# One over rms by token taken from its row through memory, and a reordering around a last projection, in a decoder layer on one core

## The chip, the core and the metric

The kernel runs on one core of one Trainium2 chip. The time is device microseconds of one execution; for before it is the median of three runs. TensorE (PE) multiplies, with its weight loads (PEld) beside it; VectorE (DVE), ScalarE (ACT) and GpSimd (POOL) work elementwise; SyncE (SP) issues most transfers, POOL and ScalarE some. Each engine runs its own queue of instructions in order and waits for others through semaphores.

## The reference

One decoder layer in float32: 512 tokens, width 1024, 256 memory tokens, FFN hidden width 2816.

```python
def rms_norm(x, g):
    var = jnp.mean(x * x, axis=-1, keepdims=True)
    return x * lax.rsqrt(var + EPS) * g

h = rms_norm(x, norm_mix)
q_a, k_a, v_a, u_b, gate_b, gate_c, g_a, g_b = split(h @ w_in)
# A: strictly causal stick-breaking attention, 8 heads of 64
# B: gate_b * causal_depthwise_conv3(gate_c * u_b)
merged = sigmoid(g_a) * (o_a @ w_branch_a) + sigmoid(g_b) * (y_b @ w_branch_b)
x = x + merged @ w_mix_out
# softmax attention over memory, 4 heads of 256
x = x + memory_cross_attention(rms_norm(x, norm_mem_q), rms_norm(mem, norm_mem_kv), ...)
gate, up = split(rms_norm(x, norm_ffn) @ w_ffn_in)
x = x + (silu(gate) * up) @ w_ffn_out
return rms_norm(x, norm_final)
```

There are five norms: first (mixer), memory, second (queries to the memory), third (FFN) and final. In the kernel 1/rms is not multiplied into the activations. It stays out of the matmuls and is applied to their results.

## The kernel before, in words

Activations lie turned, channels on partitions and tokens along the free dimension: 8 tiles of 128x512. To keep float32 accuracy every operand of a matmul is split into a high part in fp32r (made by a cast on ScalarE, or on VectorE at attention's weights) and the low rest (a subtraction on VectorE), and a product is three matmuls: high·high, high·low, low·high. The names end in `h` and `l`: `wh`, `wl` for weights from a raw tile `wr` (`load_w`), `xgh`, `xgl` for activations times the norm's gain. A weight tile passes through SyncE's load, ScalarE's cast and VectorE's subtraction; the pools have four buffers of each, so the next cast waits until TensorE has left an older tile.

**Norms.** Squares are added up per channel tile on VectorE into `acc` (`acc0`, `accm` for the memory). `squares_mean` splits `acc` into `acch` and `accl` and gives two ways to the mean over the channels, both by a matmul with the matrix `mean_r`: `along` yields the mean of every token along a row, the same on all partitions (`varb`, two matmuls of 128x512, or 128x256 for the memory), and `by_token` yields one column per 128 tokens, tokens on partitions (`var`, two matmuls of 128x2 per 128 tokens: eight, or four for the memory). `rstd_of` makes 1/rms of it by Ln and Exp on ScalarE and one Newton step on VectorE. The first norm uses both: the row `r0b` scales projections that lie turned, the column `r0` scales v, whose tokens lie on partitions. The memory norm uses both (`rm`, `rmb`), the second only a column `r1`, the third a row, that `turn_r2` also turns into a column `rt` for the final stage: POOL stores the row to DRAM and loads it back as four columns.

**Order of the work.** v of all tokens (L260), `stacked` splits v; then stick-breaking attention in steps, with projections, convolution, gates, memory norm (at step MEAN_AT) and memory projections as filling; per step `scores` makes z, `weights` the exponent `a` and its split `ah`, `al` (L385, L386), `values` multiplies by v. POOL masks `e` and `a` (L329). Then the branch projections `br` and the mixed output (`residual`, tiles `r`), which also makes x1's activations, their squares and `mean1`. While `residual` and what follows run, POOL adds four parts of FFN output weights (`pre`, L467, `weight_sums`); its first loads wait for a copy of x1's first activation. Then per memory head: `mem_q` (two query tiles `mq` of 24 matmuls each), scores `sc`, softmax with `r1s`, `om`; `residual` again; then the FFN.

The FFN's up and gate products are done by a scheme of seven products per hidden tile pair (banks z, v, y; weights `wf`), and so is the output projection (tiles `p`, weights `w01`, `w23`, `w46` and `wq`, forms `f01`, `fh`, `f26`, `f45` of the hidden activations). `second` makes `sb` from y and frees y's bank; `evict` multiplies by the row of the third norm (part 0), applies Silu (1), multiplies gate and up (2). `out_cast` loads and casts a weight, `rest_of` makes its low part, `out_pair` does both. In the last loop of the projection each iteration has six or more products per pair (`run`), the next weights, and one of eight output tiles from `groups`: its residual is turned by TensorE (`turned`), and one iteration later `settle` adds it on VectorE; for the tiles (0,0) and (1,0), `l`, ScalarE squares them right then.

In the FFN's stages the order on TensorE, ScalarE and VectorE is the order in the code. Before them a scheduler orders each engine's queue, from the code's order and the dependences.

Of the kernel before, what the change touches and what calls it, by code (L numbers as in the profile page):

```python
# [13 lines left out]
P = 128  # L14
# [29 lines left out]
def hybrid_layer(ctx: ExitStack, tc: tile.TileContext, xT_d, memT_d, cols_d, wv_d, win_d,  # L44
# [28 lines left out]
    def f(ap):  # L73
        return ap.bitcast(F32)
# [7 lines left out]
    def otile(s):  # L82
        return mmtile(s, po, "o")
# [92 lines left out]
    def squares_mean(acc, n):  # L176

        parts = unit("acch", n * P), unit("accl", n * P)
        nc.vector.tensor_copy(parts[0], acc)
        nc.vector.tensor_tensor(out=parts[1], in0=acc, in1=f(parts[0]), op=ALU.subtract)  # L180

        def by_token(s, tables=()):

            vp = otile("var")
            for t in range(n):
                for i in range(2):
                    nc.tensor.matmul(vp[:, 2 * t:2 * t + 2], parts[i][:, t * P:(t + 1) * P],
                                     mean_r[:, 0:2], start=i == 0, stop=i == 1)
            return rstd_of(vp[:, 0:2 * n].rearrange("p (t two) -> p t two", two=2)[:, :, 0], n, s,
                           tables)  # L190

        def along(s, tables=(), bank=otile):

            vp = bank("varb")[:, :n * P]
            for i in range(2):
                nc.tensor.matmul(vp, mean_r, parts[i], start=i == 0, stop=i == 1)
            return rstd_of(vp, n * P, s, tables)

        return by_token, along


    xg, wv = [], []
    acc0 = tmp("acc")
# [33 lines left out]
        lead.append(square)  # L237
    mean0 = squares_mean(acc0, TT)

    def stacked(src, scale, odd):  # L240
# [5 lines left out]
        nc.scalar.activation(hi, src, AF.Copy, scale=scale)  # L246
        nc.vector.scalar_tensor_tensor(out=lo, in0=src, scalar=scale, in1=f(hi), op0=ALU.mult,
                                       op1=ALU.subtract)
        return u


# [1 line left out]
    for k in range(KD):  # L253

        terms = ((0, 0), (0, 1), (1, 0))
        for some in ((term,) for term in terms) if k == 0 else (terms,):
            for t in range(TT):
                sl = slice(t * P, (t + 1) * P)
                for a, b in some:
                    nc.tensor.matmul(vps[t], xg[k][a][:, sl], wv[k][b],  # L260
                                     start=k == 0 and (a, b) == (0, 0),
                                     stop=k == KD - 1 and a == 1)
    r0b, r0 = mean0[1]("r0b"), mean0[0]("r0")
    v = [[stacked(vps[t], r0[:, t:t + 1], h) for h in range(2)] for t in range(TT)]


    def project(col):
# [101 lines left out]
    def weights(p, kt):  # L369
        c0, n, d = span(kt)  # L370
        av[p, kt] = []
        for h in range(2):
            z = zs[p, kt][h][:, :n]
            if kt < TT - 1:
                off = span(kt + 1)[0] - c0
                for part in rest[p, kt, h]:
                    nc.tensor.matmul(z[:, off:], neg1, part, start=False, stop=False,
                                     skip_group_check=True)
            for part in sp[p, kt, h]:
                nc.tensor.matmul(z, negtri, part, start=False, stop=True, skip_group_check=True)  # L380
# [4 lines left out]
            nc.vector.tensor_copy(ah, a)  # L385
            nc.vector.tensor_tensor(out=al, in0=a, in1=f(ah), op=ALU.subtract)  # L386
            av[p, kt].append((ah, al))

    def values(p, kt):
# [48 lines left out]
    for i in range(len(steps) + 1):  # L438
        if i in MEM_AT:
            mem_square(MEM_AT.index(i))  # L440
        if i == MEAN_AT - 4:
            mean = squares_mean(accm, MT)
        if i == MEAN_AT:
            rm, rmb = mean[0]("rm"), mean[1]("rmb")
        while fill and n_fill - len(fill) < (i + 1) * n_fill / len(steps):
            g, *args = fill.pop(0)
            g(*args)
        if i + 1 < len(steps):
            scores(*steps[i + 1])
        if i < len(steps):  # L450
            weights(*steps[i])
        if i > 0:
            values(*steps[i - 1])
# [148 lines left out]
    def mem_q(h):  # L602
        got = []
        for j in range(2):
            w = load_w(wmq_d[2 * h + j])
            ps = mmtile("mq")
            gemm(ps, w, x1g)
            got.append(split(ps, "mq"))
        return got

    q_next = mem_q(0)
    r1 = mean1[0]("r1", log_exp_tables(sigmoid))
    r1s = cpool.tile([P, TT], F32, tag="r1s", name="r1s")
    nc.vector.tensor_scalar(out=r1s, in0=r1, scalar1=(D // MH) ** -0.5, scalar2=None, op0=ALU.mult)
    for h in range(MH):
# [173 lines left out]
    rt = cpool.tile([P, TT], F32, tag="rt", name="rt")  # L789
    nrt = cpool.tile([P, TT], F32, tag="nrt", name="nrt")  # L790

    def turn_r2():

        row = dpool.tile([1, S], F32, tag="row", name="row")
        nc.gpsimd.dma_start(row, r2b[0][0:1, :])
        nc.gpsimd.dma_start(rt, row.rearrange("o (t p) -> p (o t)", p=P))
        nc.gpsimd.tensor_scalar(out=nrt, in0=rt, scalar1=-1.0, scalar2=None, op0=ALU.mult)

    forms, ows = {}, {}

# [98 lines left out]
    def w01(j):  # L899
        return j, wq(j), 0, 1  # L900
# [20 lines left out]
    with tc.manual_schedule(engines={mybir.EngineType.PE, mybir.EngineType.Activation,  # L921
# [6 lines left out]
        for n, (m, i) in enumerate(uses):  # L928
            if (m, i) == (1, 0):
                product(banks[m]["z"], m, i, range(KP - 1, KP))  # L930
            elif n > 2:
                product(bank_of(m, i), m, i)
            if i == 4:
                reads(m, i)
            else:
                if i == 1 and m > 0:
                    second(m - 1)
                reads(m, i)
            if n + AHEAD < len(uses):
                ffn_form(*uses[n + AHEAD])  # L940
            if n + AHEAD + SUM_AHEAD < len(uses):
                ffn_raw(*uses[n + AHEAD + SUM_AHEAD])
            if (m, i) == (0, 6):
                r2b[0] = mean2[1]("r0b", bank=mmtile)
                turn_r2()

            if i == 0 and m > 1:
                evict(m - 2, 0)
            elif i == 4 and 0 < m < NF - 1:
                evict(m - 1, 1)  # L950
            elif i == 1 and m > 1:
                evict(m - 2, 2)
            if (m, i) == (NF - 2, 6):
                evict(m, 0)
                evict(m, 1)
                x3 = half_form(3, 0, 0)
# [97 lines left out]

        def onto(out_, p, t, old, sign=1):
            nc.vector.scalar_tensor_tensor(out=out_, in0=p,
                                           scalar=(rt if sign > 0 else nrt)[:, t:t + 1], in1=old,
                                           op0=ALU.mult, op1=ALU.add)

        ys = {}  # L1060
# [39 lines left out]
        for j in range(NJ - 2):  # L1100
            run(4, j)
            if j == 0:
                uv = [plus("uv", res[2][s2], u[s2]) for s2 in range(2)]
                res[5] = [ztile("p5") for _ in range(2)]
            settle()
            act_third(j + 2)
            run(6, j)
            out_pair(*w46(j + 2))
            if 0 < j < BEHIND + 1:
                run(5, j - 1)  # L1110
            out_one(j + 1)
            if j < len(groups):
                pending.append((*groups[j], turned(*groups[j])))
# [137 lines left out]
```

## Time and profile before

| | |
|---|---|
| median of three runs | 862.02 us (861.31 to 862.38) |
| profiled execution | 862.09 us, of which 860.4 us span |
| granted TensorE clock | 0.998 |
| TensorE busy | 846.9 us, 98% |
| VectorE busy | 656.9 us, 76% |
| ScalarE busy | 460.2 us, 53% |
| POOL busy | 152.2 us, 18% |
| moved by DMA | 139.54 MB, mean 162 GB/s |

A row of the profile names the engine, the line of the kernel, the operation, and the tiles that it writes and reads (`out<-in`). In a view in time the first number is the start in us and the second the length; brackets at the end give how long the engine had stood idle before the instruction, and what ended that. Matmuls overlap: a 128x512 one is listed with 0.39 us, yet the next starts 0.227 us later, so a gap is read from starts. "Chain" is the chain of work that ended last, followed back from the end through whatever released each step.

### The profile page before, as it was taken

What the parts mean: (1) busy time and instruction counts of PE and PEld (TensorE: products, weight loads), DVE (VectorE), ACT (ScalarE), POOL (GpSimd) and SP (SyncE); (2) the same over time, 40 slices, a digit from 0 to 9 for tenths busy, and PEclk for the clock granted to TensorE, in tenths of its full rate; (3) what the DMA queues carried; (4) which work ended last, traced back from release to release, by engine and by line L of the source; (5) the groups of instructions that cost most, each with busy time, mean ns of one, the idle gap of its engine ahead of it and who ended that gap; (6) DMA issues with size and microseconds to landing.
All of it is one profiled execution on the core that took longest, in us unless ns stands there. A gap on an engine that the chain in (4) does not pass through costs nothing.

```text
span 860.4 us, 12842 instructions
## 1 busy us (share of the span) xinstructions
PE 846.9 (98%) x4840; PEld 737.6 (86%) x4840; DVE 656.9 (76%) x1082; ACT 460.2 (53%) x846; POOL 152.2 (18%) x183
## 2 busy tenths in 40 slices
PE   9999999999999999999999999999999999999995
PEld 7878888887888889888888789999999999888884
DVE  7768898986665766577555689888887888899877
ACT  7566676666332354533344566654455555576644
POOL 0021221111556540064000011111111110000001
PEclk9999999999999999999999999999999999999999
DMA  8332212225588766566441435767777773366542
GB/s 294 122 111 86 86 62 74 74 75 171 202 297 304 283 231 197 172 237 238 135 111 50 103 74 140 186 173 183 184 181 189 189 178 97 127 227 204 171 167 98
DMA packets 48574, 139.54 MB, mean 162 GB/s; under 512 B 4608, under 2 KB 6656, under 8 KB 45696
## 3 DMA queue, kind: packets, MB, share of 16 engines
q1 hardware_dynamic: 39008, 103.82, 36.6%
q0 software_dynamic: 9216, 34.61, 15.4%
q8 instruction: 38, 0.62, 0.3%
q10 hardware_dynamic: 288, 0.28, 0.1%
q14 instruction: 24, 0.20, 0.1%
HBM read 125.07 MB, written 13.63 MB: 161 GB/s over the span
## 4 chain that ended last, share of the span: by engine, by line
PE 95%; DVE 3%; ACT 1%; issue 1%; POOL 0%; ACTq 0%; DVEq 0%; POOLq 0%
PE z L727 15%; PE p L992 9%; PE pr L155 8%; PE pr L154 8%; PE pr L156 8%; PE y L727 7%; PE v L727 4%; PE r L155 3%; PE r L156 3%; PE r L154 3%; PE v L260 3%; PE br L154 2%; PE mq L156 2%; PE br L155 2%; PE mq L155 2%; PE mq L154 2%
## 5 line engine op out<-in xcount | busy, mean ns | idle before, releaser
L149 ACT CAST wh<-wr 128x1024 fp32r<-128x1024 f32 x84 | 88.0, 1052 | 165.4 <-issue 73.0
L150 DVE TENSOR_TENSOR wl<-wr,wh 128x1024 fp32r<-128x1024 f32 x84 | 110.4, 1316 | 36.7 <-ACT wh L149 36.6
L155 PE MATMUL pr<-xgl,wh 128*128 128x512 f32 x288 | 112.4, 390 | 0.0
L154 PE MATMUL pr<-xgh,wh 128*128 128x512 f32 x288 | 112.3, 390 | 0.0
L156 PE MATMUL pr<-xgh,wl 128*128 128x512 f32 x288 | 112.2, 390 | 0.0
L467 POOL TENSOR_TENSOR pre<-pre 128x512 f32<-128x512 f32 x44 | 71.8, 1636 | 33.7 <-DMA pre<-in_w_ffn_out_dram 31.4
L696 POOL DMA_DIRECT2D ws<-in_w_ffn_in_dram x22 | 26.5, 1206 | 256.1 <-DVE wf L717 122.9
L727 PE MATMUL z<-xdh,wf 128*128 128x256 f32 x352 | 70.5, 283 | 0.2 <-ACT sb L748 0.2
L156 PEld LDWEIGHTS pr<-xgh,wl 128*128 128x128 f32 x288 | 54.1, 188 | 11.2
L154 PEld LDWEIGHTS pr<-xgh,wh 128*128 128x128 f32 x288 | 54.1, 188 | 11.0
L155 PEld LDWEIGHTS pr<-xgl,wh 128*128 128x128 f32 x288 | 54.1, 188 | 11.0
L748 ACT COPY sa<-z 128x256 f32<-128x256 f32 x44 | 16.4, 372 | 79.3 <-PE z L727 78.4
L727 PEld LDWEIGHTS z<-xdh,wf 128*128 128x128 f32 x352 | 58.0, 192 | 0.5 <-ACT sb L748 0.4
L717 DVE TENSOR_TENSOR wf<-s,wf 128x512 fp32r<-128x512 f32 x44 | 30.3, 691 | 25.7 <-ACT wf L716 25.6
L727 PE MATMUL z<-xdl,wf 128*128 128x256 f32 x176 | 49.8, 283 | 0.0
L810 DVE TENSOR_TENSOR wl<-wr,wh 128x1024 fp32r<-128x1024 f32 x33 | 40.3, 1223 | 4.7 <-ACT wh L877 4.7
L877 ACT CAST wh<-wr 128x1024 fp32r<-128x1024 f32 x33 | 34.5, 1049 | 6.4 <-DMA wr<-sums 4.3
L727 PE MATMUL y<-xoh,wf 128*128 128x256 f32 x176 | 35.4, 284 | 0.7 <-DVE sb L758 0.7
L727 PE MATMUL z<-xch,wf 128*128 128x256 f32 x176 | 35.4, 284 | 0.1
L727 PE MATMUL y<-xch,wf 128*128 128x256 f32 x176 | 35.4, 283 | 0.0
L727 PE MATMUL v<-xoh,wf 128*128 128x256 f32 x176 | 35.4, 283 | 0.0
L727 PE MATMUL z<-xf,wf 128*128 128x256 f32 x264 | 35.4, 283 | 0.0
(333 smaller groups left out, 2422.3 us busy)
## 6 DMA issues: line engine op xcount, KB each, us to landing
wr<-in_w_in_dram SPq DMA_DIRECT2D x36, 512.0 KB, 3.5
pre<-in_w_ffn_out_dram POOLq DMA_DIRECT2D x11, 1024.0 KB, 8.5
sums<-pre POOLq DMA_DIRECT2D x11, 1024.0 KB, 4.9
ws<-in_w_ffn_in_dram SPq DMA_DIRECT2D x22, 512.0 KB, 3.7
wg<-in_w_ffn_in_dram SPq DMA_DIRECT2D x22, 512.0 KB, 4.3
ws<-in_w_ffn_in_dram POOLq DMA_DIRECT2D x22, 512.0 KB, 6.3
wr<-sums SPq DMA_DIRECT2D x22, 512.0 KB, 4.5
wr<-in_w_ffn_out_dram SPq DMA_DIRECT2D x16, 512.0 KB, 4.0
```

Of the source, the lines that this page charges most:

```text
L149: after(nc.scalar.copy(h2, raw), lead[-1:])
L150: lows.append(nc.vector.tensor_tensor(out=l2, in0=raw, in1=f(h2), op=ALU.subtract))
L154: nc.tensor.matmul(ps, a[0], b[0], start=start, stop=False, **kw)
L155: nc.tensor.matmul(ps, a[0], b[1], start=False, stop=False, **kw)
L156: nc.tensor.matmul(ps, a[1], b[0], start=False, stop=stop, **kw)
L467: nc.gpsimd.tensor_tensor(out=t[:, a, :], in0=t[:, a, :], in1=t[:, b, :], op=ALU.add)
L696: nc.gpsimd.dma_start(s13, a[:, 0:4:3, :], accum_op=ALU.add)
L717: nc.vector.tensor_tensor(out=w[:, 1, :], in0=raw, in1=f(w[:, 0, :]), op=ALU.subtract)
L727: nc.tensor.matmul(ps[:, :HS], a, b, start=i < 3 and k == 0 and j == 0, stop=k == KP - 1 and j == 2, skip_group_check=True)
L810: nc.vector.tensor_tensor(out=lo, in0=src, in1=f(hi), op=ALU.subtract)
L877: nc.scalar.copy(hi, raw)
L992: nc.tensor.matmul(res[i][s2], a[:, ts], b, start=j == 0 and n == 0, stop=j == NJ - 1 and n == 2)
```

## The change

1. `by_token` goes. `squares_mean` now gives `along` and a new `turned`, which copies the row of means with ScalarE, stores it to DRAM and loads it back as columns (both on SyncE), and makes 1/rms of the columns. The common part is `turned_row`.
2. First norm: only the row is made, and `r0` is read from `r0b` by POOL's two transfers. v is split without it; `r0` is multiplied into attention's weights, where `ah` becomes a TENSOR_SCALAR and `al` a SCALAR_TENSOR_TENSOR.
3. Memory norm: the same, `rm` from `rmb` by two transfers of POOL.
4. Second norm: `turned`, and it is called ahead of `mem_q(0)`, where the column was made behind it.
5. End of the gate and up products: `second` of the last tile ahead of `rest_of` of weights and form; `out_cast` of both `w23` weights and some half forms earlier; the last `w23`'s `rest_of` ahead of the last `evict`.
6. Last loop: `groups` starts with (0,0) and (1,0), and `settle` stands behind `out_pair` and `run(6, j)`.

```diff
-        def by_token(s, tables=()):
-
-            vp = otile("var")
-            for t in range(n):
-                for i in range(2):
-                    nc.tensor.matmul(vp[:, 2 * t:2 * t + 2], parts[i][:, t * P:(t + 1) * P],
-                                     mean_r[:, 0:2], start=i == 0, stop=i == 1)
...
+        def turned(s, tables=(), bank=otile):
+
+            row = tmp("vrow")
+            nc.scalar.copy(row[0:1, :n * P], mean(bank)[0:1, :])
+            return rstd_of(turned_row(row[0:1, :n * P], n, "v" + s, nc.sync, nc.sync), n, s, tables)
...
+    def turned_row(row, n, s, store, load):
+
+        d = dpool.tile([1, n * P], F32, tag="row" + s, name=nm("row"))
+        store.dma_start(d, row)
+        t = cpool.tile([P, n], F32, tag=s, name=nm(s))
+        load.dma_start(t, d.rearrange("o (t p) -> p (o t)", p=P))
+        return t
...
-    r0b, r0 = mean0[1]("r0b"), mean0[0]("r0")
-    v = [[stacked(vps[t], r0[:, t:t + 1], h) for h in range(2)] for t in range(TT)]
+    v = [[stacked(vps[t], h) for h in range(2)] for t in range(TT)]
+    r0b = mean0[0]("r0b")
+    r0 = turned_row(r0b[0:1, :], TT, "r0", nc.gpsimd, nc.gpsimd)
...
-            nc.vector.tensor_copy(ah, a)
-            nc.vector.tensor_tensor(out=al, in0=a, in1=f(ah), op=ALU.subtract)
+            r = r0[:, kt:kt + 1]
+            nc.vector.tensor_scalar(out=ah, in0=a, scalar1=r, scalar2=None, op0=ALU.mult)
+            nc.vector.scalar_tensor_tensor(out=al, in0=a, scalar=r, in1=f(ah), op0=ALU.mult,
+                                           op1=ALU.subtract)
...
-            rm, rmb = mean[0]("rm"), mean[1]("rmb")
+            rmb = mean[0]("rmb")
+            rm = turned_row(rmb[0:1, :], MT, "rm", nc.gpsimd, nc.gpsimd)
...
+    r1 = mean1[1]("r1", log_exp_tables(sigmoid))
     q_next = mem_q(0)
-    r1 = mean1[0]("r1", log_exp_tables(sigmoid))
...
             if (m, i) == (NF - 2, 6):
+                w, x3 = out_cast(*w23(0)), half_form(3, 0, 0)
                 evict(m, 0)
                 evict(m, 1)
-                x3 = half_form(3, 0, 0)
                 rest_of(*x3)
+                x2 = half_form(2, 1, 0)
             if (m, i) == (NF - 1, 5):
                 evict(NF - 2, 2)
-                out_pair(*w23(0))
-                x2 = half_form(2, 1, 0)
+                rest_of(*w)
                 rest_of(*x2)
                 n2_of(x2[0], 1)
+                x3 = half_form(3, 1, 0)
...
                 w, x = out_cast(*w01(1)), cast_first(1)
+                x2 = half_form(2, 0, 0)
+                second(NF - 1)
                 rest_of(*w)
                 rest_of(*x)
-                x2 = half_form(2, 0, 0)
-                second(NF - 1)
                 rest_of(*x2)
                 n2_of(x2[0], 0)
+        w = out_cast(*w23(1))
         evict(NF - 1, 0)
         evict(NF - 1, 1)
-        x3 = half_form(3, 1, 0)
-        w = out_cast(*w23(1))
         rest_of(*x3)
+        rest_of(*w)
         evict(NF - 1, 2)
-        rest_of(*w)
...
-        groups = [(2, 0), (2, 1), (3, 0), (3, 1), (0, 1), (1, 1), (0, 0), (1, 0)]
+        groups = [(0, 0), (1, 0), (2, 0), (2, 1), (3, 0), (3, 1), (0, 1), (1, 1)]
...
+            act_third(j + 2)
+            out_pair(*w46(j + 2))
+            run(6, j)
             settle()
-            act_third(j + 2)
-            run(6, j)
-            out_pair(*w46(j + 2))
```

What stands in a queue now. TensorE at the second norm: before, the column's matmuls behind the last ones of the second query tile, and ahead of the scores `sc`:

```order
L154 MATMUL mq825_3965<-xgh805_3883,wh823_3961 128x512
L155 MATMUL mq825_3965<-xgl806_3884,wh823_3961 128x512
L156 MATMUL mq825_3965<-xgh805_3883,wl824_3962 128x512
L187 MATMUL var828_3995<-mean_r_100,acch808_3890 128x2
L187 MATMUL var828_3995<-mean_r_100,accl809_3891 128x2
L187 MATMUL var828_3995<-mean_r_100,acch808_3890 128x2
```

After, the row's two matmuls within the first query tile:

```order
L156 MATMUL mq821_3924<-xgh775_3734,wl820_3921 128x512
L154 MATMUL mq821_3924<-xgh783_3775,wh819_3920 128x512
L155 MATMUL mq821_3924<-xgl784_3776,wh819_3920 128x512
L185 MATMUL varb811_3900<-acch802_3864,mean_r_100 128x512
L156 MATMUL mq821_3924<-xgh783_3775,wl820_3921 128x512
L154 MATMUL mq821_3924<-xgh791_3816,wh819_3920 128x512
L155 MATMUL mq821_3924<-xgl792_3817,wh819_3920 128x512
L185 MATMUL varb811_3900<-accl803_3865,mean_r_100 128x512
L156 MATMUL mq821_3924<-xgh791_3816,wl820_3921 128x512
L154 MATMUL mq821_3924<-xgh799_3857,wh819_3920 128x512
```

The first stands behind 17 of that tile's 24 matmuls, and the scores follow the second tile directly.

VectorE at the end of the gate and up products: before, `wl` and `f01l` are the two weights and forms of the first products of `p`, `sb` is the work of `second(NF - 1)`:

```order
L810 TENSOR_TENSOR wl_7855<-wr_7852,wh_7854 128x1024
L810 TENSOR_TENSOR f01l_7858<-a_5288,f01h_7857 128x512
L810 TENSOR_TENSOR wl_7890<-wr_7887,wh_7889 128x1024
L810 TENSOR_TENSOR f01l_7893<-a_5555,f01h_7892 128x512
L758 TENSOR_TENSOR sb_7765<-y_7823,sb_7765 128x256
L810 TENSOR_TENSOR fh_7897<-a_5289,fh_7897 128x256
```

After:

```order
L819 TENSOR_TENSOR wl_7829<-wr_7826,wh_7828 128x1024
L819 TENSOR_TENSOR f01l_7832<-a_5262,f01h_7831 128x512
L769 TENSOR_TENSOR sb_7739<-y_7797,sb_7739 128x256
L819 TENSOR_TENSOR wl_7864<-wr_7861,wh_7863 128x1024
L819 TENSOR_TENSOR f01l_7867<-a_5529,f01h_7866 128x512
L819 TENSOR_TENSOR fh_7869<-a_5263,fh_7869 128x256
```

`sb` moved ahead of the second `wl` and `f01l`. A dozen rows on, the last `w23` weight's `wl` has moved ahead of the two products of `evict` (`a`), which before were its predecessors.

ScalarE in the last iterations of the projection's last loop: before, `sq` is the square of an `l` tile, `f45h`, `wh` and `wq` are casts of a form and of weights:

```order
L892 CAST wq_8795<-wr_8756 128x512
L1063 ACTIVATE sq_8810,ss<-l_8478 128x512
L806 CAST f45h_8813<-a_7691 128x512
L877 CAST wh_8825<-wr_8823 128x1024
L892 CAST wq_8837<-wr_8835 128x512
L1063 ACTIVATE sq_8852,ss<-l_8480 128x512
L806 CAST f45h_8855<-a_7932 128x512
L877 CAST wh_8867<-wr_8865 128x1024
L892 CAST wq_8871<-wr_8835 128x512
```

After:

```order
L901 CAST wq_8775<-wr_8736 128x512
L815 CAST f45h_8789<-a_7665 128x512
L886 CAST wh_8795<-wr_8793 128x1024
L901 CAST wq_8814<-wr_8812 128x512
L815 CAST f45h_8828<-a_7913 128x512
L886 CAST wh_8834<-wr_8832 128x1024
L901 CAST wq_8845<-wr_8812 128x512
```

The two squares are gone from here; they now stand in the loop's first iterations, each behind a `wh`.

More of the change, by code (lines that the diff above doesn't have):

```diff
@@ L180, in squares_mean, with mean @@
         nc.vector.tensor_tensor(out=parts[1], in0=acc, in1=f(parts[0]), op=ALU.subtract)
-        def by_token(s, tables=()):
-            vp = otile("var")
-            for t in range(n):
-                for i in range(2):
-                    nc.tensor.matmul(vp[:, 2 * t:2 * t + 2], parts[i][:, t * P:(t + 1) * P],
-                                     mean_r[:, 0:2], start=i == 0, stop=i == 1)
-            return rstd_of(vp[:, 0:2 * n].rearrange("p (t two) -> p t two", two=2)[:, :, 0], n, s,
-                           tables)
-        def along(s, tables=(), bank=otile):
+        def mean(bank):
             vp = bank("varb")[:, :n * P]
@@ L196, in along @@
                 nc.tensor.matmul(vp, mean_r, parts[i], start=i == 0, stop=i == 1)
+            return vp
+        def along(s, tables=(), bank=otile):
+            vp = mean(bank)
             return rstd_of(vp, n * P, s, tables)
-        return by_token, along
+        def turned(s, tables=(), bank=otile):
+            row = tmp("vrow")
+            nc.scalar.copy(row[0:1, :n * P], mean(bank)[0:1, :])
+            return rstd_of(turned_row(row[0:1, :n * P], n, "v" + s, nc.sync, nc.sync), n, s, tables)
+        return along, turned
+    def turned_row(row, n, s, store, load):
[4 more added lines that the diff above has]
+        return t
     xg, wv = [], []
@@ L238, in hybrid_layer, with stacked @@
     mean0 = squares_mean(acc0, TT)
-    def stacked(src, scale, odd):
+    def stacked(src, odd):
         u = unit("v").rearrange("p (a s d) -> p a s d", s=2, d=HD)
@@ L245, in stacked @@
         src = src.rearrange("p (a b d) -> p a b d", b=2, d=HD)[:, :, odd, :]
-        nc.scalar.activation(hi, src, AF.Copy, scale=scale)
-        nc.vector.scalar_tensor_tensor(out=lo, in0=src, scalar=scale, in1=f(hi), op0=ALU.mult,
-                                       op1=ALU.subtract)
+        nc.scalar.copy(hi, src)
+        nc.vector.tensor_tensor(out=lo, in0=src, in1=f(hi), op=ALU.subtract)
         return u
@@ L788, in hybrid_layer @@
     r2b = [None]
-    rt = cpool.tile([P, TT], F32, tag="rt", name="rt")
+    rt = []
     nrt = cpool.tile([P, TT], F32, tag="nrt", name="nrt")
     def turn_r2():
[L794 to L797, printed above, removed]
+        rt.append(turned_row(r2b[0][0:1, :], TT, "rt", nc.gpsimd, nc.gpsimd))
+        nc.gpsimd.tensor_scalar(out=nrt, in0=rt[0], scalar1=-1.0, scalar2=None, op0=ALU.mult)
     forms, ows = {}, {}
@@ L943, in hybrid_layer @@
             if (m, i) == (0, 6):
-                r2b[0] = mean2[1]("r0b", bank=mmtile)
+                r2b[0] = mean2[0]("r0b", bank=mmtile)
                 turn_r2()
@@ L1056, in onto @@
             nc.vector.scalar_tensor_tensor(out=out_, in0=p,
-                                           scalar=(rt if sign > 0 else nrt)[:, t:t + 1], in1=old,
+                                           scalar=(rt[0] if sign > 0 else nrt)[:, t:t + 1], in1=old,
                                            op0=ALU.mult, op1=ALU.add)
```

## The prediction, on record before the result

> **What bounds the kernel now.** I read the page first: the span, and the chain of work that ended last, by engine.
>
> ```profile
> span 860.4 us, 12842 instructions
> ...
> PE 95%; DVE 3%; ACT 1%; issue 1%; POOL 0%; ACTq 0%; DVEq 0%; POOLq 0%
> ```
>
> TensorE carries 95% of the chain, so time comes only from matmuls that go, or from TensorE's waits. The second view is the table of TensorE's waits (total, times, longest, us):
>
> ```profile
> PE p L992 <- DVE wl L810: 1.1, 2, 0.9
> PE y L727 <- DVE sb L758: 0.7, 1, 0.7
> PE br L154 <- DVE g L503: 0.5, 1, 0.5
> ```
>
> Behind the start these are nearly all: under 3 us. The first two lie where the change reorders work. Third, the chain in order of time (start, length), at the small matmuls that the change removes:
>
> ```profile
> 28.21 0.79 PE var L187 x8
> ...
> 174.49 0.57 PE var L187 x4
> ...
> 412.45 0.79 PE var L187 x8
> ```
>
> The profiled execution took 862.09 us, 860.4 of span and 1.69 around it. That is 0.07 above the median 862.02: I sum against 862.09 and take 0.07 off at the end. About 0.2%, 1.72 us, is what a measurement of this kernel can tell from no change.
>
> **The change part by part.** *First norm and memory norm.* The matmul behind a removed group also starts late, as TensorE's rows show at the first group, which stands between the first two of these:
>
> ```profile
> 27.82 0.40 PE L196 MATMUL varb<-accl,mean_r 128*128 128x512 f32 x1
> ...
> 28.86 0.47 PE L154 MATMUL pr<-xgh,wh 128*128 128x512 f32 x1
> 29.18 0.39 PE L155 MATMUL pr<-xgl,wh 128*128 128x512 f32 x1
> 29.41 0.40 PE L156 MATMUL pr<-xgh,wl 128*128 128x512 f32 x1
> ```
>
> 29.18 to 29.41 is the undisturbed step, 0.23. From 27.82 to 29.18 are 1.36 for two such steps: the eight cost 1.36 − 0.46 = 0.90. Four, with the chain's 0.57, about 0.60. Together **−1.50**. The rows' matmuls stay; they were computed already.
>
> In their place stand two transfers each on POOL's queue. The kernel has one such pair (last number: median us from issue to landing):
>
> ```profile
> row<-r0b POOLq DMA_DIRECT2D x1, 2.0 KB, 3.8
> rt<-row POOLq DMA_DIRECT2D x1, 2.0 KB, 4.1
> ```
>
> With what lies between I take 8.3 us for a pair. A load of weights on SyncE's queue takes 3.4 alone:
>
> ```profile
> wr<-in_w_mem_o_dram SPq DMA_DIRECT2D x8, 512.0 KB, 3.4
> ```
>
> r0's row should be ready at about 33 us (VectorE now splits v ahead of it, some 1.5 us more than before), r0 at 41.6. Its first reader is the first split of attention weights; and POOL's next work after rm's transfers is a mask:
>
> ```profile
> 56.33 0.38 DVE L385 CAST ah<-a 128x256 fp32r<-128x256 f32 x1
> ```
>
> ```profile
> 186.92 0.29 POOL L329 TENSOR_SCALAR_AFFINE_SELECT e<-e 128x128 f32<-128x128 f32 x1 [12.96 <-DVE e L356]
> ```
>
> r0 has 14 us of cover: cost nothing. rm's row should be ready at 180.3 and holds POOL until its load is issued, some 5.0 us, to 185.3. The mask behind it, earlier by about 0.9 for the matmuls gone, is due at 186.0. A margin of 0.7, and two more until TensorE wants what follows: cost nothing, up to 1 if the store is late.
>
> r0 in the weights' split turns a cast into TENSOR_SCALAR and a subtraction into SCALAR_TENSOR_TENSOR. The page's kind of groups, by form (busy, mean ns), has both kinds at one size:
>
> ```profile
> L308 DVE SCALAR_TENSOR_TENSOR cv<-cu,gcol,cv 128x512 f32<-128x512 f32 x8 | 6.0, 751 | 0.2
> L386 DVE TENSOR_TENSOR al<-a,ah 128x512 fp32r<-128x512 f32 x8 | 5.8, 724 | 0.2
> L385 DVE CAST ah<-a 128x512 fp32r<-128x512 f32 x8 | 3.6, 453 | 2.9 <-POOL a L329 2.9
> L304 DVE TENSOR_SCALAR cv<-cu,gcol 128x512 f32<-128x512 f32 x4 | 1.9, 483 | 0.0
> ```
>
> 27 and 30 ns more. For 32 pairs that is 32 × 0.057 = 1.8 us of VectorE, double if small tiles pay more, spread over 150 us of attention in which TensorE waits for VectorE for some 0.7 us in all (br's 0.5 the largest). I take 0, and ±0.2 for the range.
>
> *Second norm.* The column's eight go: −0.90. A row of two 128x512 matmuls comes: +0.46. But the first of these now stands behind 17 of the first query tile's 24 matmuls, where the column stood behind two whole tiles. TensorE's and VectorE's rows:
>
> ```profile
> 401.41 0.39 PE L154 MATMUL mq<-xgh,wh 128*128 128x512 f32 x1
> ```
>
> ```profile
> 398.21 0.75 DVE L172 SCALAR_TENSOR_TENSOR xgl<-x,gcol,xgh 128x512 fp32r<-128x512 f32 x1
> ...
> 402.51 1.75 DVE L150 TENSOR_TENSOR wl<-wr,wh 128x1024 fp32r<-128x1024 f32 x1 [0.21 <-ACT wh L149]
> 404.18 1.78 DVE L172 SCALAR_TENSOR_TENSOR xgl<-x,gcol,xgh 128x512 fp32r<-128x512 f32 x1
> ...
> 406.60 0.43 DVE L179 CAST acch<-acc 128x512 fp32r<-128x512 f32 x1
> ```
>
> TensorE reaches the row at 401.41 + 17 × 0.227 (the 0.23 above in one digit more) = 405.27; its operand acch ends at 407.03. The work up to there is in the same order in both kernels. So TensorE stands **1.75 us** where it had not stood. What makes VectorE late is seen in the two forms of one instruction, 0.75 at 398.21 and 1.78 at 404.18; POOL adds weights just then:
>
> ```profile
> 398.69 6.72 POOL L467 TENSOR_TENSOR pre<-pre 128x512 f32<-128x512 f32 x4 [8.00 <-DMA pre<-in_w_ffn_out_dram]
> ```
>
> POOL's adds start from a copy of this stage's first activation, so they move along with it and I expect them in the same place. Without them VectorE would be 0.5 + 1.0 earlier and the wait about 0.2: the ends are 0.2 and 1.9, and I take the upper, whose rows are those of this place.
>
> The Trainium skill ("SBUF — State Buffer", section "Who interferes with whom") says that a VectorE instruction with two SBUF inputs and a GpSimd instruction that reads SBUF exclude each other for the whole instruction, whichever issued first. The trace agrees: 1.78 against 0.75 while POOL adds. By this rule, too, the wait stays as long as the two meet.
>
> Then r1 itself. These rows of ScalarE and TensorE set who asks for it:
>
> ```profile
> 412.31 1.05 ACT L149 CAST wh<-wr 128x1024 fp32r<-128x1024 f32 x1 [3.91 <-issue]
> 413.26 0.58 ACT L168 CAST mqh<-mq 128x512 fp32r<-128x512 f32 x1
> 413.74 0.27 ACT L123 ACTIVATE ry<-var,eps_t 128x4 f32<-128x4 f32 x1
> ```
>
> ```profile
> 414.60 0.28 PE L154 MATMUL sc<-kmh,mqh 128*128 128x256 f32 x1
> ```
>
> After, ry stands ahead of this mqh, and waits for r1's load. In before's times the second tile now ends at 401.41 + 48 × 0.227 + 0.46 + 1.75 = 414.5; wh until 415.6, ry until 415.85, mqh until 416.4. The scores want it after six small and four large matmuls more, at 416.2 (before they had it from 413.84 for 414.60): 0.2 us of wait from ry alone. The load: the row is copied at 409.0 and stored; the load back stands in SyncE's queue behind a weight load that goes out when VectorE's next wl is done, near 411.6. So it is issued at 412.0 and, by the two landings quoted above, is there at 415.8 to 416.1, against 415.6: 0.2 to 0.5 more at the slow end, nothing where SyncE's queue is quicker than POOL's. I take 0.2 for it. Second norm: −0.90 + 0.46 + 1.75 + 0.40 = **+1.71**.
>
> The Trainium skill ("DMA: Bandwidth & Descriptors", section "Anatomy of one DMA — SWDGE (gpsimd) path") puts the fixed part of one DMA at about 2.0 us. By this the load is in time, and the sum would be 0.2 lower; the trace's 3.8 and 4.1 decide.
>
> *Last gate and up tiles.* VectorE's sb, which frees a bank, stood behind a weight's subtraction and a form's. Its rows, and TensorE's around its wait:
>
> ```profile
> 738.60 0.42 DVE L758 TENSOR_TENSOR sb<-y,sb 128x256 f32<-128x256 f32 x1
> ...
> 748.41 2.35 DVE L810 TENSOR_TENSOR wl<-wr,wh 128x1024 fp32r<-128x1024 f32 x2
> ```
>
> ```profile
> 738.07 0.28 PE L727 MATMUL z<-xdh,wf 128*128 128x256 f32 x1
> 739.08 0.39 PE L727 MATMUL y<-xoh,wf 128*128 128x256 f32 x1 [0.73 <-DVE sb L758]
> ...
> 749.69 0.50 PE L992 MATMUL p<-wl,fh 128*128 128x512 f32 x1 [0.27 <-DVE wl L810]
> ```
>
> Now sb goes first. What it reads, the tile's third product and ScalarE's copy of the fifth, is there before the last z products end, so it no longer ends last. TensorE goes on at 738.07 + 0.12 = 738.19: −0.89. The wl of 748.41 (first of two) now stands ahead of the SwiGLU products, and its cast ahead of a sigmoid: done near 748.05, wanted at 749.69 − 0.43 − 0.89 = 748.37. The wait before 749.69, 0.43 by the step between matmuls (0.27 idle and a slow start), goes as well. Next late is the following wl, with 0.9 to spare. **−1.32**; if the wl were 0.5 later than I think, −1.1.
>
> *Last projection.* In the final iterations the squares of two output tiles stood ahead of the last casts, and waited for VectorE's addition. ScalarE, VectorE, TensorE:
>
> ```profile
> 837.86 0.63 ACT L1063 ACTIVATE sq<-l 128x512 f32<-128x512 f32 x1 [2.38 <-DVE l L1056]
> ```
>
> ```profile
> 840.43 1.21 DVE L810 TENSOR_TENSOR wl<-wr,wh 128x1024 fp32r<-128x1024 f32 x1
> ```
>
> ```profile
> 840.44 0.39 PE L992 MATMUL p<-wh,f45h 128*128 128x512 f32 x1
> 841.69 0.50 PE L992 MATMUL p<-wl,f45h 128*128 128x512 f32 x1 [0.86 <-DVE wl L810]
> ```
>
> The last wl is wanted at 840.44 + 0.23 = 840.67 and came a microsecond late. Now these two squares run in the first iterations, where weights lie more than 6 us ahead, and the last casts follow the freed slots: wl near 838.4. 841.69 − 840.67 = **−1.02**, and the end moves with TensorE.
>
> Sum: −1.50 + 1.71 − 1.32 − 1.02 = −2.13. 862.09 − 2.13 − 0.07 = **859.9 us**.
>
> **The rivals.** *(1) VectorE is not late at r1's row.* POOL's adds fall elsewhere, or are done: the wait is 0.2 and its followers keep their margin. −2.13 − 1.55 − 0.2 = −3.9: 858.1. For it: transfers of 8 us decide when POOL starts. Against: they move with the stage.
>
> *(2) r1's way through memory sets the pace.* From the store to r1 in place I allow 6.6 us (409.0 to 415.6). Every us beyond holds ScalarE's and VectorE's queues, and so the scores. The pair on POOL took 8.3: +1.7, less the 0.2 already counted, 861.4, within 0.2%. From about 8.9 us the change is slower than before: at 11 us, which one more 512 KB load of 3.4 us ahead in the queue would make, 8.3 + 3.4 being 11.7 where none of it overlaps, −2.13 + 4.2 = +2.1: 864.1. For it: SyncE's queue carries large loads. Against: SyncE doesn't need POOL's preparation.
>
> *(3) The reordering at the end does not pay.* If the casts there wait for weights' transfers and not for the squares, 1.02 stays, and perhaps the 0.43: −0.7 to −1.1, 861.0 to 861.3. Against: in the rows before, ScalarE's idle time there ends on VectorE.
>
> *(4) Attention feels VectorE's 1.8 to 3.5 us or POOL's blocked queue:* +1 at most beside the rest, 860.9.
>
> **How the numbers follow.** Forecast 0.45 (859.2 to 860.6 by its own bounds), (1) 0.2, (2) 0.17 (0.1 within 0.2%, 0.07 slower), (3) 0.1, (4) 0.08. Faster by over 0.2% means below 860.3: (1) and three quarters of the forecast, 0.54, with a little of (3) and (4), 0.58. Slower: (2)'s far half and a little for small losses that add up, 0.09. The rest, 0.33, lies within 0.2%. The range runs from (1)'s 858.1, a little below, to (2)'s near half: 857.9 to 861.8.
>
> **What would show it.** Right: no var groups on the chain at 28, 174 and 412; a TensorE wait of varb on VectorE's acch, 1.5 to 2 us, near 404, with wl and xgl at 1.7; a small one of sc on mqh; no wait of y on sb, and none of p on wl behind 735. Wrong: acch ready first (rival 1), sc waiting over 1 us behind ry (2), p still waiting near 840 (3), or new waits in attention (4).

## The result, and the profile after

The changed kernel takes 860.24 us (median of 18 runs, 859.49 to 860.81), before 861.79 (18 runs, 861.31 to 862.76): ratio 0.998, 95% interval 0.9973 to 0.9987. That is 1.55 us or 0.18%: faster, clear of noise by its interval, and just inside the 0.2% that the prediction counts as no change. The prediction was 859.9, 2.1 us faster, and it had given its largest chance, 0.58, to a gain above 0.2%; what came is the outcome to which it gave 0.33. The profiled execution took 860.42 us, of which 858.7 span; against before's 860.4 the span is 1.7 shorter.

The page of after, its span and the chain that ended last by engine:

```profile
span 858.7 us, 12803 instructions
...
PE 95%; DVE 3%; ACT 1%; issue 1%; POOL 0%; ACTq 0%; POOLq 0%
```

TensorE's waits after (total, times, longest, us):

```profile
PE varb L185 <- DVE acch L179: 1.8, 1, 1.8
PE warm L227 <- DVE neg L91: 1.4, 1, 1.4
PE br L154 <- DVE g L514: 0.5, 1, 0.5
```

The waits of y on sb and of p on wl are gone, and one new wait, as long as these together, has come: that on acch. (`warm` stands at the start of the program, and before has the same 1.4.) TensorE's, VectorE's and POOL's rows in time at that place:

```profile
403.62 0.39 PE L155 MATMUL mq<-xgl,wh 128*128 128x512 f32 x1
405.76 0.47 PE L185 MATMUL varb<-acch,mean_r 128*128 128x512 f32 x1 [1.75 <-DVE acch L179]
406.06 0.40 PE L156 MATMUL mq<-xgh,wl 128*128 128x512 f32 x1
```

```profile
401.10 1.75 DVE L150 TENSOR_TENSOR wl<-wr,wh 128x1024 fp32r<-128x1024 f32 x1 [0.21 <-ACT wh L149]
402.77 1.77 DVE L172 SCALAR_TENSOR_TENSOR xgl<-x,gcol,xgh 128x512 fp32r<-128x512 f32 x1
...
405.19 0.43 DVE L179 CAST acch<-acc 128x512 fp32r<-128x512 f32 x1
```

```profile
397.16 6.84 POOL L478 TENSOR_TENSOR pre<-pre 128x512 f32<-128x512 f32 x4 [8.06 <-DMA pre<-in_w_ffn_out_dram]
```

VectorE's wl and xgl are again 0.5 and 1.0 longer than undisturbed, in the stretch in which POOL adds. TensorE stands from 403.62 + 0.23 to 405.76, 1.91 us, and loses another 0.07 on the next step.

How far TensorE is ahead of before can be read from starts of the same matmul in both traces. It shows in which stage the time came or went:

| start of | before | after | difference |
|---|---|---|---|
| first projection `pr` | 28.86 | 27.80 | −1.06 |
| first query tile `mq` | 401.41 | 399.99 | −1.42 |
| first `om` of the memory | 429.73 | 430.12 | +0.39 |
| first product `p` | 740.62 | 740.00 | −0.62 |
| the 50th `p` | 752.56 | 751.56 | −1.00 |
| the 420th `p`, last loop | 840.22 | 839.32 | −0.90 |
| the 441st `p`, last loop | 846.15 | 844.08 | −2.07 |
| issue of the last store | 856.64 | 854.61 | −2.03 |
| end of the span | 860.4 | 858.7 | −1.7 |

Between the 50th and the 420th `p` 0.1 is lost over 88 us of the same work. The last two rows are SyncE's. By the rows here the end lies 3.76 us behind the last store's issue before, and 4.09 after; with the span not rounded to a tenth, 3.74 and 4.11. So 0.37 us that TensorE had won is lost behind the issue of the last store. I call this stretch the closing.

### The profile page after: what moved, and what is told of

Read it like the earlier page. It is cut to its first block, busy times and chain, and to the rows that moved or that the text cites. A ratio compares the mean times of both kernels' runs of the same rounds, so it can differ in the third digit from the quotient of the medians.

```text
span 858.7 us, 12803 instructions
## 1 busy us (share of the span) xinstructions
PE 844.8 (98%) x4822; PEld 735.7 (86%) x4822; DVE 657.7 (77%) x1074; ACT 459.7 (54%) x843; POOL 153.7 (18%) x187
## 4 chain that ended last, share of the span: by engine, by line
PE 95%; DVE 3%; ACT 1%; issue 1%; POOL 0%; ACTq 0%; POOLq 0%
PE z L738 15%; PE p L1001 10%; PE pr L155 8%; PE pr L156 8%; PE pr L154 8%; PE y L738 7%; PE v L738 4%; PE r L154 3%; PE r L155 3%; PE r L156 3%; PE v L267 3%; PE br L154 2%; PE br L155 2%; PE br L156 2%; PE mq L156 2%; PE mq L154 2%
```

## The experiments

Eight kernels ran, each timed beside before on the same chip. Before took 862.13 there; the intervals of the ratios are some ±0.13% wide for five runs, ±0.09% for eleven, so the stages are read from the traces and the times confirm them.

**undo_r1: the second norm put back.** `by_token` is there again as the third of the functions, and is called behind the query tiles:

```diff
-    r1 = mean1[1]("r1", log_exp_tables(sigmoid))
     q_next = mem_q(0)
+    r1 = mean1[2]("r1", log_exp_tables(sigmoid))
```

> The changed kernel with the second norm put back: a column from eight small matmuls behind the first two query tiles. In the traces the second norm as changed costs 1.79 us (TensorE 1.42 ahead of before at the first query tile, 0.37 behind it at the FFN). If that is its whole price, this version is 1.8 us faster than the changed kernel, so about 3.3 us faster than before: near 858.4, and no TensorE wait on acch is left. Rival, that the row saves TensorE work here as at the other norms: 0.4 slower than the changed kernel or more, above 860.6.

858.38 us, ratio 0.9958 (0.9945 to 0.9970): 3.75 faster than before where the change is 1.55 faster. No wait on acch is left. TensorE's lead from `mq` to `om` stays at 0.75. So the change without its second norm is about 2 us better, more than the 1.8 of TensorE's rows. The closing is part of the rest: it is 3.74 here, as before; why, the last experiment shows. The rival is out.

**r1_behind: the row later.**

```diff
-    r1 = mean1[1]("r1", log_exp_tables(sigmoid))
     q_next = mem_q(0)
+    r1 = mean1[1]("r1", log_exp_tables(sigmoid))
```

> The changed kernel with r1's row called behind the first two query tiles instead of ahead of them; the row's two matmuls then stand directly ahead of the scores, 7 us after acch is made. If the price of the second norm is the wait for acch (1.91 us by the step between matmuls) and not the round trip through memory, this is about 2.0 us faster than the changed kernel: near 858.2, with no wait on acch. Rival, that r1's way through memory sets the pace: r1 then arrives near 419 where the softmax asks for it near 417, it holds ScalarE's and VectorE's queues, TensorE waits up to 2 us at the scores or at the next query tile, and the time stays near 860.2.

858.77 us, ratio 0.9961 (0.9948 to 0.9975). The row stands ahead of the scores and waits for nothing, and r1 arrives as late as expected, as VectorE's first step on it shows:

```profile
411.32 0.39 PE L156 MATMUL mq<-xgh,wl 128*128 128x512 f32 x1
411.55 0.39 PE L185 MATMUL varb<-acch,mean_r 128*128 128x512 f32 x1
```

```profile
415.69 1.53 DVE L642 TENSOR_REDUCE mx<-sc 128x2 f32<-128x512 f32 x2 [1.22 <-PE sc L156]
418.69 0.17 DVE L124 TENSOR_SCALAR rv<-vr 128x4 f32<-128x4 f32 x1 [1.46 <-DMA vr<-row]
```

TensorE has no wait for it: the softmax's probabilities are used later still. In the trace TensorE's lead grows from 0.74 at `mq` to 1.09 at `om`, so the row in place of the column is worth 0.35 (the forecast had 0.44). The price of the second norm was the wait for acch, not the way through memory. The time is 0.6 above the 858.2 expected, within its interval, and not below undo_r1's: in the traces the 0.35 that the row saves on TensorE is lost again in the closing, which is 4.11 here as in the change.

**sums_early: POOL's additions moved away.**

```diff
-    weight_sums(range(SUMS_FIRST, NJ), x1g[0][0])
+    weight_sums(range(SUMS_FIRST, NJ), vm[1][1][0])
```

> The changed kernel with POOL's additions of weights gated by an earlier tile (the memory's last v tile in place of the first activation of this stage), so that they begin and end some 6.5 us earlier; nothing else moves. If POOL's additions make VectorE late at r1's row, the last tile's wl and xgl fall to 1.23 and 0.75, TensorE's wait on acch falls from 1.8 to 0.3 or less, and the time is 1.6 to 1.9 below the changed kernel: near 858.5. If VectorE is late by its own order, the wait stays at 1.8 and the time at 860.2.

858.57 us, ratio 0.9962 (0.9949 to 0.9974). POOL's last additions, VectorE's last tile and TensorE's row now:

```profile
386.26 6.66 POOL L478 TENSOR_TENSOR pre<-pre 128x512 f32<-128x512 f32 x4 [6.99 <-DMA pre<-in_w_ffn_out_dram]
```

```profile
400.64 1.23 DVE L150 TENSOR_TENSOR wl<-wr,wh 128x1024 fp32r<-128x1024 f32 x1 [0.21 <-ACT wh L149]
401.78 0.75 DVE L172 SCALAR_TENSOR_TENSOR xgl<-x,gcol,xgh 128x512 fp32r<-128x512 f32 x1
```

```profile
403.73 0.47 PE L185 MATMUL varb<-acch,mean_r 128*128 128x512 f32 x1 [0.19 <-DVE acch L179]
```

POOL is done by 392.9, wl and xgl take 1.23 and 0.75, and the wait falls from 1.75 to 0.19. The order on TensorE is the same as in the change. So it is POOL that made VectorE late, and VectorE that made TensorE wait. The transfers of these weights moved along with the additions; the next run separates the two.

**r1_twice: a third transfer for r1.**

```diff
+            d = dpool.tile([1, n * P], F32, tag="once" + s, name=nm("once"))
+            nc.sync.dma_start(d, row[0:1, :n * P])
-            return rstd_of(turned_row(row[0:1, :n * P], n, "v" + s, nc.sync, nc.sync), n, s, tables)
+            return rstd_of(turned_row(d, n, "v" + s, nc.sync, nc.sync), n, s, tables)
```

> The changed kernel with r1's row taken through memory by three transfers in place of two (a second copy from memory to memory on SyncE's queue). In the changed kernel r1 is there at 413.85 and ScalarE asks for it at 414.31. A third transfer of about 3 us makes it late by 2.5: if ScalarE's and VectorE's queues stand behind r1 as the order says, TensorE waits that long at the scores and the time is 2.2 to 2.8 above the changed kernel, near 862.7. If r1's users have slack of their own, less than 0.5 above it.

A miss: 859.98 us, ratio 0.9977 (0.9968 to 0.9986), not slower than the change. The order was not the same. ScalarE's cast of the query tile now stands ahead of r1's step, where the change has it behind:

```profile
413.48 0.58 ACT L168 CAST mqh<-mq 128x512 fp32r<-128x512 f32 x1
415.17 0.30 ACT L123 ACTIVATE ry<-vr,eps_t 128x4 f32<-128x4 f32 x1 [1.11 <-DMA vr<-row]
```

So what a late r1 costs with the change's own order stays open; in the order that the scheduler chose here it cost nothing. Nor was r1 as late as planned: ScalarE waited 1.1 for it, not 2.5. The run tells something else. Its order on TensorE is the change's, but the wait on acch was 0.39:

```profile
404.90 0.47 PE L185 MATMUL varb<-acch,mean_r 128*128 128x512 f32 x1 [0.39 <-DVE acch L179]
```

POOL had waited 4.2 us for its first weights (first row) where it waited 6.8 in the trace of the change (second row):

```profile
370.62 8.38 POOL L480 TENSOR_TENSOR pre<-pre 128x512 f32<-128x512 f32 x5 [4.21 <-DMA pre<-in_w_ffn_out_dram]
```

```profile
372.72 9.18 POOL L478 TENSOR_TENSOR pre<-pre 128x512 f32<-128x512 f32 x5 [6.82 <-DMA pre<-in_w_ffn_out_dram]
```

So its last additions ended sooner, at 401.94, and VectorE's instructions behind that are short again. POOL's and VectorE's rows:

```profile
394.92 7.02 POOL L480 TENSOR_TENSOR pre<-pre 128x512 f32<-128x512 f32 x4 [8.73 <-DMA pre<-in_w_ffn_out_dram]
402.24 0.57 POOL L482 DMA_DIRECT2D sums<-pre  x1 [0.30 <-POOL pre L480]
```

```profile
397.30 1.78 DVE L172 SCALAR_TENSOR_TENSOR xgl<-x,gcol,xgh 128x512 fp32r<-128x512 f32 x1
...
401.60 1.43 DVE L150 TENSOR_TENSOR wl<-wr,wh 128x1024 fp32r<-128x1024 f32 x1 [0.21 <-ACT wh L149]
402.95 0.74 DVE L172 SCALAR_TENSOR_TENSOR xgl<-x,gcol,xgh 128x512 fp32r<-128x512 f32 x1
```

The two `xgl` are the same instruction on two tiles: 1.78 while POOL adds, 0.74 once it is done. The second runs while 1 MB of sums, whose store was issued at 402.24, is on its way, so it is the additions that stretch VectorE's work and not these transfers. The wait depends on when a transfer lands, and is not a constant of the order. Every trace tells how late acch is: its end against the start of the first `mq` plus 17 steps, the point at which the changed order asks for it. It is 1.76 late in four traces (before, after, undo_r1, ab_only), 1.43 in two (r1_behind, best), 0.85 in e_only, 0.78 in d_only, 0.40 here, and 0.20 in sums_early. The sooner POOL is done, the smaller it is.

**ab_only, d_only, e_only: one part at a time.** ab_only is the change with points 4, 5 and 6 put back; d_only is before with point 5; e_only is before with point 6.

> Only the first and the memory norm of the change; the second norm, the reordering at the end of gate and up and the last loop as before. By the traces these two norms gave 1.42 us by the first query tile. Theory: 1.3 to 1.6 faster than before, near 860.6. Rival, that r0's and rm's transfers or VectorE's longer split of attention's weights eat part of it: less than 1.0, with new TensorE waits between 40 and 212.

> Only the reordering at the end of the gate and up products. By the traces TensorE gained 1.37 us between the last z products and the second w23 weight. Theory: 1.3 to 1.4 faster than before, near 860.7, no wait of y on sb, the one of p on wl near 840 still there. Rival, that the gain came from TensorE being later there by the second norm's wait: less than 1.0.

> Only the last loop's new order of groups, and settle behind the casts. By the traces TensorE gained 1.18 us there. Theory: 1.0 to 1.2 faster than before, near 861.0, no wait of p on wl near 840, the end as far behind the last store's issue as before (3.76 us). Rival, that the tail behind TensorE takes part of it back: 0.8 or less.

| | time, us | ratio (95%) | against 862.13 | TensorE's rows |
|---|---|---|---|---|
| ab_only | 860.83 | 0.9986 (0.9977 to 0.9995) | −1.30 | −1.02 at `mq` |
| d_only | 860.42 | 0.9981 (0.9972 to 0.9990) | −1.71 | −1.42 from `mq` to the 50th `p` |
| e_only | 860.86 | 0.9987 (0.9978 to 0.9996) | −1.27 | −1.18 in the last loop |

Each is faster by itself, by about what its stage shows, though the intervals are as wide as 0.8 us to each side. ab_only is at the lower end of what was expected, and its rows show less still: the 1.42 of the change's trace was in part an early start of the first projection. The three add up to 4.3 by the times and 3.6 by the rows; undo_r1, which is all three, has 3.75. The closing of all three is before's, 3.69 to 3.75. TensorE's waits in d_only and e_only show whose they were:

```profile
PE p L992 <- DVE wl L810: 0.9, 1, 0.9
```

```profile
PE y L727 <- DVE sb L758: 0.7, 1, 0.7
...
PE p L992 <- DVE wl L810: 0.3, 1, 0.3
```

In d_only the wait of the last loop is left, in e_only the two of the gate's end.

**best: the row later, its transfers on POOL's queue.**

```diff
-    r1 = mean1[1]("r1", log_exp_tables(sigmoid))
     q_next = mem_q(0)
+    r1 = mean1[1]("r1", log_exp_tables(sigmoid))
...
-            return rstd_of(turned_row(row[0:1, :n * P], n, "v" + s, nc.sync, nc.sync), n, s, tables)
+            return rstd_of(turned_row(row[0:1, :n * P], n, "v" + s, nc.gpsimd, nc.gpsimd), n, s, tables)
```

> The changed kernel with r1's row called behind the first two query tiles, as in r1_behind, and its two transfers on POOL's queue in place of SyncE's. In the changed kernel and in r1_behind the span ends 4.1 us after the last store's issue; in before, and with the second norm put back, 3.75. Theory: the two added transfers on SyncE's queue shift which semaphores the last stores count on, and SyncE's closing waits then have more left to do behind the last landing. Then the 0.35 goes here, with TensorE as in r1_behind: 0.3 to 0.4 faster than r1_behind, near 858.2 where before takes 861.8 to 862.1. Rival, that the 0.35 belongs to the row or to memory: span again 4.1 behind the last store.

858.09 us, ratio 0.9953 (0.9941 to 0.9966): 4.0 faster than before, the lowest median here, and 0.7 below r1_behind where 0.3 to 0.4 were expected. The last store's rows of before, of after and of this kernel, with spans of 860.4, 858.7 and 855.8:

```profile
856.64 0.33 SPq L1162 DMA_DIRECT2D out_dram<-u  x1
```

```profile
854.61 0.33 SPq L1171 DMA_DIRECT2D out_dram<-u  x1
```

```profile
852.10 0.33 SPq L1171 DMA_DIRECT2D out_dram<-u  x1
```

3.76, 4.09, 3.7 by these rows, and 3.74, 4.11, 3.73 unrounded. With r1's two transfers off SyncE's queue the closing is as short as before. The medians of r1_behind and this kernel differ by 0.7, their traces' spans by 1.3: 0.38 of that is the closing, 1.0 the start of the first projection, which comes sooner here by scatter.

In the traces SyncE closes the program with a row of waits, one about every 0.06 us, on the counters of its transfers, always in one order. Before, the wait that lasts until the stores have landed stands near the end of that row, and one is left behind it; after, it stands third, and seven are left: six more, 0.37. Two more transfers on the queue shift which counters the last stores get. The stores themselves do not land later: the last landing comes 2.77 us behind the issue of SyncE's last store in both traces. r1_twice, with three transfers more than before on SyncE's queue, has six waits left and a closing of 4.08. That the added transfers on SyncE's queue lengthen the closing is shown by this run and by undo_r1 (3.74 in its trace); that they do it through the order of the waits, each costing its 0.06 in series, is read from the records.

## Why the prediction was right, and where its terms were off

Term by term, by the table of starts (us):

| term | forecast | trace of after | |
|---|---|---|---|
| first norm | −0.90 | −1.06 | right; 0.1 to 0.2 is scatter |
| memory norm | −0.60 | −0.3 to −0.4 | half |
| second norm | +1.71 | +1.81 | mechanism shown, the size in part luck |
| end of gate and up | −1.32 | −1.39 | right |
| last loop | −1.02 | −1.17 | right |
| closing | 0 | +0.37 | not foreseen |

The first and memory norms' forecast of 1.50 stands against 1.42 here. But the first number hides scatter: over ten traces the first `pr` starts between 27.34 and 28.60 without the column and between 28.66 and 28.96 with it. Most of it comes from the first microseconds. TensorE's first steps of 128x512 are 0.43 us apart, and 0.227 from about the time at which the trace records the full granted clock. That time is 4.23 in sums_early and 7.60 in undo_r1, and the first matmuls of v show it (undo_r1, then sums_early; four in a row):

```profile
5.04 2.04 PE L277 MATMUL v<-wvh,xgh 128*128 128x512 f32 x4
6.88 1.43 PE L277 MATMUL v<-wvl,xgh 128*128 128x512 f32 x4
```

```profile
5.02 1.16 PE L267 MATMUL v<-wvh,xgh 128*128 128x512 f32 x4 [0.22 <-ACT acc L242]
6.02 1.08 PE L267 MATMUL v<-wvl,xgh 128*128 128x512 f32 x4
```

Without the column the starts follow it: 4.23, 5.27, 6.04, 6.85, 6.99 and 7.60 go with 27.34, 27.46, 27.80, 28.28, 28.28 and 28.60. Only r1_behind (4.84 and 28.47) does not; there TensorE waited for VectorE's split of the first weights. Before has 6.42 and 28.86, after 6.04 and 27.80. Read at the same time of the clock, the column's removal is worth 0.8 to 0.9, an estimate from these pairs: the forecast's size.

The memory norm's 0.60 was mis-sized: in all seven traces with it TensorE gains 0.25 to 0.4 between 115 us and the first query tile. The row moved to the place where the column had stood. Its matmuls before, and then after:

```profile
177.98 0.40 PE L156 MATMUL pr<-xgh,wl 128*128 128x512 f32 x1
178.21 0.28 PE L196 MATMUL varb<-acch,mean_r 128*128 128x256 f32 x1
178.33 0.28 PE L196 MATMUL varb<-accl,mean_r 128*128 128x256 f32 x1
178.44 0.40 PE L154 MATMUL pr<-xgh,wh 128*128 128x512 f32 x1
```

```profile
172.98 0.39 PE L154 MATMUL pr<-xgh,wh 128*128 128x512 f32 x1
173.41 0.38 PE L185 MATMUL varb<-acch,mean_r 128*128 128x256 f32 x1
173.63 0.28 PE L185 MATMUL varb<-accl,mean_r 128*128 128x256 f32 x1
```

The first starts 0.43 behind the matmul ahead of it, where before it was 0.23, and the second 0.22 behind the first, where it was 0.12. So 0.3 of what the four matmuls had cost is paid again. The prediction left that out: it said that the row's matmuls were computed already.

POOL's transfers cost TensorE nothing, as forecast. rm's store and load and the mask behind them:

```profile
180.25 0.54 POOL L205 DMA_DIRECT2D row<-rmb  x1 [7.19 <-DVE rmb L129]
182.14 0.75 POOL L207 DMA_DIRECT2D rm<-row  x1 [1.35 <-DMA row<-rmb]
185.41 0.28 POOL L337 TENSOR_SCALAR_AFFINE_SELECT e<-e 128x128 f32<-128x128 f32 x1 [2.52 <-DVE e L364]
```

POOL was held from 180.25 to 182.89, 2.6 us and not 5.0, and the margin before the mask was 2.5 and not 0.7. Attention's longer splits cost VectorE 3.1 us (28.9 before, 32.0 after), more than the 1.8 of the sum and within its double. They left no new wait; `br` waits 0.5 as before.

At the second norm the main step held: 1.75 of wait, from VectorE's two stretched instructions. That it held to the digit is in part luck: of the nine traces in which the additions wait for this stage, four have 1.76, and the others 0.40 to 1.43.

Rival 1 did not come about in the profiled execution of the change, but its mechanism was right, as sums_early and, by chance, r1_twice showed: with POOL done sooner the wait is 0.2 to 0.4. Against it the prediction held that the additions move with the stage. The issue of their loads does, 35.15 us ahead of the first `mq` in all nine; the first addition, which waits for the landing, stands 26.9 to 29.9 ahead. Rival 1's price was too good: its sum has TensorE 0.04 ahead at this norm, in sums_early it loses 0.31 (its lead falls from 1.88 at `mq` to 1.57 at `om`), with 0.15 at the scores and the late start behind the wait still there.

Rival 2 did not come about: r1 was there before it was asked for. SyncE's issue, VectorE's first use, ScalarE's, and the scores:

```profile
410.66 0.42 SPq L207 DMA_DIRECT2D vr<-row  x1
```

```profile
413.85 0.17 DVE L124 TENSOR_SCALAR rv<-vr 128x4 f32<-128x4 f32 x1 [3.01 <-DMA vr<-row]
```

```profile
414.31 0.29 ACT L123 ACTIVATE ry<-vr,eps_t 128x4 f32<-128x4 f32 x1
```

```profile
414.75 0.40 PE L154 MATMUL mq<-xgh,wh 128*128 128x512 f32 x1
415.13 0.39 PE L154 MATMUL sc<-kmh,mqh 128*128 128x256 f32 x1
```

The load took 3.2 us and was 0.46 early, so the 0.2 that the sum had for a late load was not there. The 0.2 for the step of r1 ahead of the query tile's cast was: the next scores start 0.38 behind the matmul before them where a step is 0.23. r1_twice, where the cast stands ahead of r1's step, has 0.24 there. The restart behind the wait, 1.98 lost by the steps where the idle time is 1.75, made up for the difference.

Rivals 3 and 4 fell: in the last loop the last wl starts at 836.27 and is not waited for, and no wait of attention grew.

What failed is one sentence of the last step: "the end moves with TensorE". TensorE's lead at the end is 2.07, the span has 1.7. SyncE's added transfers cost 0.37 at a place where no instruction of the change stands. That 2.07 lies so close to the forecast sum of 2.13 is luck too: the memory norm gave some 0.3 too little and the second norm cost 0.1 more, and the first norm's early start, the end of gate and up and the last loop made up for it.

## What to carry to other kernels

A matmul that is moved ahead in TensorE's queue must be held against the time at which its operand is made, at that place and with what slows the maker there: 0.9 us of small matmuls were bought off with a wait of 1.9, and the same row six microseconds later had none. Where the operand's engine shares time with POOL, read one instruction's duration with and without POOL before trusting a margin. Sum a change to the end of the span and not to the last matmul: what is queued behind the last store is part of the time. And a wait that hangs on when a transfer lands has a range: one trace gives one value of it.

## What was not expected of the hardware

- Two transfers added on SyncE's queue in the middle of the program lengthened its end by 0.37 us (3.74 to 4.11 behind the last store's issue), and moving them to POOL's queue took that back (3.73).
- The same 2 KB row stored by POOL landed in 1.8 us near 33 us, in all seven traces that store it there, and in 3.3 to 5.2 us near 535 us, in all ten. The prediction took its price, 3.8, from the second place for the first. The column loaded back took 2.1 to 4.1.
- The start of the first projection differs by up to 1.26 us between traces of kernels whose code up to there is the same, mostly with the time at which TensorE's steps fall from 0.43 to 0.227 us (4.2 to 7.6 us into the program). Differences below that are better read from a later start against an earlier one of the same trace.
